# Modulation columns finished inside the large matmul loops, and filler matmuls with sink copies at four transitions of a two-block kernel

## The chip, the cores and the metric

One program runs on one core of a Trainium2 chip. The metric is the device time of an execution in microseconds (us); three executions of the kernel before took 2094.62, 2098.63 and 2100.15 us, so the median is 2098.63 us.

## The reference

Two transformer blocks stand behind each other, on one sequence of 256 tokens with 1024 features, all in float32. Each block first makes six modulation vectors of 1024 numbers from a conditioning vector, and uses them as shift, scale and gate:

```
mod = c @ w_mod + b_mod                # block 2: silu(c_2) @ w_ada_2 + b_ada_2
sh1, sc1, gt1, sh2, sc2, gt2 = split(mod, 6)
h  = rmsnorm(x, norm1_g) * (1 + sc1) + sh1
z  = h @ w_in                          # mixer: pooling, two kinds of attention, gates
x  = x + gt1 * (y @ w_out)             # y: what the mixer makes of z
h2 = rmsnorm(x, norm2_g) * (1 + sc2) + sh2
x  = x + gt2 * peer_ffn(h2)            # 16384 experts, all scored, 16 kept per head
```

Block 1 ends with a norm by `final_g`, and block 2 takes its result as `x`. So the norm at the end of block 1 and the norm at the head of block 2 follow directly on each other.

## The kernel before

The features of a token lie on the partitions in eight groups of 128 (`kk` 0 to 7). A product of two float32 matrices is made of three passes over a high and a low part of each (`hhi`, `hlo` for the activations, `hi`, `lo` for the weights), so every weight of 128x2048 that the SP queue loads into a raw buffer is split by ScalarE (L138, the high part) and VectorE (L141, the low part) before TensorE can use it. `Stream` keeps three raw buffers and three split buffers in one fixed order of units. The order of the instructions on each engine is the order in which the Python code records them: nothing is rescheduled afterwards, and every engine works through its own list in that order.

The time goes to four long stretches of matmuls: the mixer of block 1 (from 34 us to 228 us), its expert layer (235 us to 1042 us), the mixer of block 2 (1055 us to 1274 us) and its expert layer (from 1280 us). An expert layer writes the scores of the experts (`u` units, 128x256 matmuls, L442) and then the sums over them (`v` units, 128x512 matmuls, L897). Between the stretches lie four **transitions**, in which TensorE has little to do because a norm has to be worked out first:

- the **start**: `x` is loaded, normed, transposed (L552), and modulated by the first two modulation vectors into `hhi` and `hlo`;
- the **middle of block 1** and the **middle of block 2**, both at the end of `out_proj`: transposes of the new `x` (`turn`, L552), the rows' rsqrt (`norm_rows`), the spreading of it over the partitions (`spread_rows`, L516), then `modulate`, which makes eight products on VectorE (L533), eight high parts on ScalarE (L537) and eight low parts on VectorE (L524); TensorE's next matmuls (`mm_first`, L458 and L462) read them;
- the **seam of the blocks**, at the end of `peer` for block 1: the same, with two norms at once, in two groups of four `kk`, and with a new `xs` written in between (L1078); TensorE's next matmuls are L484.

A modulation vector is a sum over 1024 rows. VectorE adds the rows of the eight groups into one tile of 128x1024 (`mod_handler`, L332 and L334, tiles `macc` or `ringa`) while the weights stream by; TensorE then sums over the partitions with eight matmuls against a column of ones (`column`, L290; each is two records in the trace), and VectorE adds the bias (L300, and L303 for a scale). This last step is `finish_mod`. Finished tiles wait in the list `pending`, and `flush` takes them from its front after each unit, once they are three units old, but not those in `HOLD`, which wait for a transition (block and vector counted from 0):

```
HOLD = {(0, 3), (0, 4), (1, 1), (1, 0), (1, 2), (1, 3), (1, 4)}
while pending and pending[0][0] >= age and (age == 0 or pending[0][1] not in HOLD):
    finish_next()()
```

In the middle of block 1 two vectors are so finished, at the seam four, in the middle of block 2 one.

Of the kernel before, what the change touches and what calls it, by code (L numbers as in the profile page):

```python
# [9 lines left out]
F32 = mybir.dt.float32  # L10
# [30 lines left out]
RATE2 = 2  # L41
HOLD = {(0, 3), (0, 4), (1, 1), (1, 0), (1, 2), (1, 3), (1, 4)}

# [153 lines left out]
def kernel(  # L197
# [39 lines left out]

    # ---------------------------------------------------------- constants
    xpool = [ctx.enter_context(ExitStack())]
# [31 lines left out]

    # ---------------------------------------------------------- modulation
    modc = [keep.tile([128, 6, 8], F32, name=f"modc{b}") for b in range(2)]
# [4 lines left out]
    def mm_scratch():  # L278
        return ps_mm.tile([128, 512], F32, name="mm", tag="mm")
# [25 lines left out]

    def finish_next():
        age, bj, t, place, ps = pending.pop(0)
        del users[place]
        return finish_mod(*bj, t, ps)
# [33 lines left out]
    def flush(age=3):  # L343
        for p in pending:
            p[0] += 1
        while pending and pending[0][0] >= age and (age == 0 or pending[0][1] not in HOLD):
            finish_next()()

# [18 lines left out]

    # ---------------------------------------------------------- unit order
    last_v, first_v, xnext = [], [], []
# [55 lines left out]

    # ---------------------------------------------------------- helpers
    small = ctx.enter_context(tc.tile_pool(name="small", bufs=2))
# [48 lines left out]
    def mm_te(src, tick=None):  # L476
        ps = mm_tile()
        for p in range(2):
# [9 lines left out]
            if tick is not None:  # L488
                st.ahead()
                tick()  # L490
        return ps

    def rsqrt_seed(parts, base):
# [16 lines left out]
    def rsqrt_start(parts, base, v):  # L510
        return rsqrt_polish(rsqrt_seed(parts, base), v)
# [36 lines left out]
    def turn(xT, xs, i):  # L548
        for k in range(2):
            for tt in range(2):  # L550
                kk = 2 * i + k
                PE.transpose(xT[i][:, k, tt * 128:(tt + 1) * 128], xs[:, tt, kk * 128:(kk + 1) * 128], ident)  # L552
# [14 lines left out]
    def out_proj(b, yT, xs, gt, pool, at, rbt, ubuf):  # L567
# [37 lines left out]
        scale = finish_next()  # L605
        turn(xT, xs, tail[1])
        rb = norm_rows(ms, rbt, lambda: st.fill(2))
        scale()
        rest = [finish_next() for _ in range(len(pending))]
        modulate(b, 1, lambda kk: [(xT[kk // 2][:, kk % 2, :], slice(0, 256))], rb, ubuf,  # L610
                 first=lambda: [r() for r in rest] and rest.clear(), group=4)

    # ---------------------------------------------------------- PEER
    def peer(b, plan, keys_d, gelu, xs):
        with ExitStack() as px:
# [178 lines left out]
            with ExitStack() as gx:  # L794
# [253 lines left out]
                if b == 0:  # L1048
# [6 lines left out]
                    turn_x(1, 0)  # L1055
                    rest = [finish_next()]
                    scale()
                    turn_x(1, 1)
                    r = rsqrt_start([part[:, 0:1], part[:, 1:2]], base, v)
                    right.close()  # L1060
                    xnext.append(open_x())
                    st.fill(SPLIT_BUFS - 1)
                    rb = small.tile([128, S], F32, name="rb", tag="rb", bufs=1)
                    spread_rows(rb, r, psp.tile([128, 512], F32, name="g", tag="g"))
                    rest += [finish_next() for _ in range(len(pending))]
                    turns = [0, 1]
# [20 lines left out]

    # ---------------------------------------------------------- block 1 mixer
    with ExitStack() as mx:
# [43 lines left out]
        for _ in range(4):  # L1133
            st.process()
            st.settle()
        flush(0)
        sh, gs = modc[0][:, 0, :], modc[0][:, 1, :]
        for kk in range(8):
            A.activation(sga[:, kk, :], xT[kk // 2][:, kk % 2, :], AF.Copy, scale=gs[:, kk:kk + 1])
        for _ in range(3):  # L1140
            st.process()
            st.settle()
        st.fill(1)
        flush(0)
# [203 lines left out]

    # ---------------------------------------------------------- block 2 mixer
    with ExitStack() as mx:  # L1350
# [310 lines left out]
```

## Time and profile before

| | before |
|---|---|
| three executions, us | 2094.62, 2098.63, 2100.15 |
| median, us | 2098.63 |
| span of the profiled execution, first to last instruction, us | 2093.1 |
| median less that span, us | 5.5 |
| TensorE busy, us (share of the span) | 2050.3 (98%) |
| VectorE busy, us | 1603.1 (77%) |
| ScalarE busy, us | 986.8 (47%) |
| mean granted TensorE clock, of full speed | 0.989 |

The profile gives the span of the profiled execution and no time of its own beside it; the 5.5 us to the median stand for what lies around the span. "Busy" counts an instruction from its start to its end, and TensorE's instructions overlap, so 98% does not mean 98% of its peak. A number in brackets behind a row of the timeline is the time for which the engine had stood idle just before, with what ended the wait. The granted clock has two levels here, 1.00 (2.4 GHz) and 0.50 (1.2 GHz).

### The profile page before, as it was taken

How to read it: one execution, taken by the hardware profiler on the slowest of the kernel's cores; microseconds unless marked ns; L12 is line 12 of the kernel's file. 1: busy time of each engine (PE TensorE's matmuls, PEld its weight loads, DVE VectorE, ACT ScalarE, POOL GpSimd, SP SyncE). 2: the span in 40 equal slices, each digit the busy share in tenths (PEclk: the TensorE clock that was granted, in tenths of full speed). 3: DMA queues.
4: the chain of work that ended last, by engine and by line, in shares of the span. 5: the costliest groups of instructions: out<-in, count | busy, mean ns of one | idle time of the engine just before them, and what ended most of it. 6: DMA issues, size and time to landing. Idle time of an engine off the chain costs nothing.

```text
span 2093.1 us, 37810 instructions
## 1 busy us (share of the span) xinstructions
PE 2050.3 (98%) x15694; PEld 1885.9 (90%) x15694; DVE 1603.1 (77%) x2937; ACT 986.8 (47%) x1307; POOL 5.6 (0%) x15
## 2 busy tenths in 40 slices
PE   5999999999999999999999999999999999999998
PEld 4999999999999877888899999999999998778886
DVE  6787698868876799777668557988588766996556
ACT  4446455544344434444554455555443444344444
POOL 0000000000000000000000000000000000000000
PEclk8999999999999999999989999999999999999999
DMA  8555545554447644588445345555544475445563
GB/s 346 210 218 202 181 164 198 183 184 171 165 168 266 239 161 163 208 333 306 184 174 201 132 141 182 180 183 184 199 163 162 165 259 200 156 168 181 190 222 121
DMA packets 57211, 408.83 MB, mean 195 GB/s; under 512 B 6352, under 2 KB 6736, under 8 KB 8016
## 3 DMA queue, kind: packets, MB, share of 16 engines
q1 hardware_dynamic: 55424, 397.76, 53.4%
q0 software_dynamic: 1296, 8.52, 1.2%
q8 instruction: 123, 2.02, 0.4%
q14 instruction: 48, 0.39, 0.1%
q10 hardware_dynamic: 320, 0.14, 0.0%
HBM read 403.26 MB, written 3.15 MB: 194 GB/s over the span
## 4 chain that ended last, share of the span: by engine, by line
PE 91%; DVE 4%; ACT 2%; DMA 2%; issue 1%; SPq 0%; ACTq 0%; DVEq 0%
PE mm L442 46%; PE acc L897 31%; PE mm L484 2%; PE mm L580 2%; PE g L834 2%; PE g L835 1%; DVE lo L141 1%; PE acc L984 1%; DVE macc L334 1%; DMA raw<-in_w_in_dram 1%; ACT hi L138 1%; PE g L766 1%; PE acc L880 1%; PE mm L458 1%; PE mm L290 0%
## 5 line engine op out<-in xcount | busy, mean ns | idle before, releaser
L141 DVE TENSOR_TENSOR lo<-raw,hi 128x1024 fp32r<-128x1024 f32 x632 | 766.2, 1221 | 366.2 <-ACT hi L138 365.0
L138 ACT ACTIVATE hi<-raw 128x1024 fp32r<-128x1024 f32 x632 | 663.5, 1055 | 490.8 <-PE acc L897 226.5
L442 PE MATMUL mm<-hhi,hi 128*128 128x256 f32 x2848 | 399.8, 282 | 1.9 <-ACT sga L1330 1.6
L442 PE MATMUL mm<-hlo,hi 128*128 128x256 f32 x2848 | 392.9, 280 | 0.0
L442 PE MATMUL mm<-hhi,lo 128*128 128x256 f32 x2848 | 392.7, 280 | 0.0
L442 PEld LDWEIGHTS mm<-hhi,hi 128*128 128x128 f32 x2848 | 359.8, 188 | 6.2 <-ACT sga L1330 1.8
L442 PEld LDWEIGHTS mm<-hhi,lo 128*128 128x128 f32 x2848 | 358.0, 188 | 0.0
L442 PEld LDWEIGHTS mm<-hlo,hi 128*128 128x128 f32 x2848 | 357.9, 188 | 0.0
L897 PE MATMUL acc<-hi,whi 128*128 128x512 f32 x976 | 307.1, 396 | 0.7 <-ACT whi L545 0.7
L897 PE MATMUL acc<-lo,whi 128*128 128x512 f32 x976 | 301.9, 391 | 0.0
L897 PE MATMUL acc<-hi,wlo 128*128 128x512 f32 x976 | 300.6, 389 | 0.0
L897 PEld LDWEIGHTS acc<-hi,wlo 128*128 128x128 f32 x976 | 183.2, 188 | 39.6
L897 PEld LDWEIGHTS acc<-lo,whi 128*128 128x128 f32 x976 | 183.2, 188 | 39.1
L897 PEld LDWEIGHTS acc<-hi,whi 128*128 128x128 f32 x976 | 177.2, 188 | 33.5 <-ACT whi L545 1.6
L636 ACT ACTIVATE ringa<-mm 128x512 f32<-128x512 f32 x80 | 47.9, 599 | 111.6 <-PE mm L442 111.6
L827 DVE TENSOR_TENSOR gg<-b,gT 128x512 f16<-128x512 f16 x256 | 96.2, 417 | 0.0
L824 DVE TENSOR_TENSOR b<-iota,idx2T 128x1024 f16<-128x1024 f16 x128 | 87.5, 683 | 0.0
L545 ACT ACTIVATE whi<-ringa 128x512 fp32r<-128x512 f32 x78 | 48.8, 628 | 77.3 <-PE acc L897 77.3
L834 PEld LDWEIGHTS <-b 128*128 128x128 f16 x1024 | 63.4, 98 | 20.2 <-issue 8.3
L834 PE MATMUL g<-gg,b 128*128 128x64 f16 x1024 | 78.2, 194 | 0.1
L835 PE MATMUL g<-gg,b 128*128 128x64 f16 x1024 | 77.0, 193 | 0.0
L636 ACT ACTIVATE ringb<-mm 128x512 f32<-128x512 f32 x48 | 28.7, 599 | 93.8 <-PE mm L442 93.8
(359 smaller groups left out, 1837.5 us busy)
## 6 DMA issues: line engine op xcount, KB each, us to landing
raw<-in_peer_u_dram SPq DMA_DIRECT2D x128, 1024.0 KB, 4.9
raw<-in_peer_v_dram SPq DMA_DIRECT2D x118, 1024.0 KB, 4.9
raw<-in_w_in_dram SPq DMA_DIRECT2D x45, 1024.0 KB, 5.0
raw<-in_w_mod_dram SPq DMA_DIRECT2D x20, 1024.0 KB, 5.0
raw<-in_w_ada_dram SPq DMA_DIRECT2D x20, 1024.0 KB, 5.4
ringa<-in_peer_v_dram SPq DMA_DIRECT2D x10, 1024.0 KB, 5.6
raw<-in_w_out_dram SPq DMA_DIRECT2D x8, 1024.0 KB, 4.9
raw<-in_w_query_dram SPq DMA_DIRECT2D x8, 1024.0 KB, 4.9
```

What stands on the lines that cost most here:

```text
L138: self.nc.scalar.activation(hi, src, AF.Copy)
L141: self.nc.vector.tensor_sub(lo, src, hi.bitcast(F32))
L442: PE.matmul(ps[:, j, :], lhsT=w[:, k, :], rhs=h[:, k, :], start=n == 0 and k == 0, stop=n == 2 and k == 7)
L484: PE.matmul(ps[:, tt, :], lhsT=h[:, 4 * p + k, tt * 128:(tt + 1) * 128], rhs=w[:, k, :], start=p == 0 and tt == 0 and i == 0, stop=p == 1 ...
L545: A.activation(hi, src, AF.Copy)
L580: PE.matmul(acc[q][:, tt, :], lhsT=h[:, 4 * p + k, tt * 128:(tt + 1) * 128], rhs=w[:, k, :], start=p == 0 and tt == 0 and i == 0, stop=p = ...
L636: state["evac"] = lambda: A.activation(slots(p), ps, gelu)
L824: V.tensor_tensor(pairs(b2), lanes(0, 128), each(idx2T[:, c], 128), op=OP.is_equal)
L827: V.tensor_tensor(pairs(gg[:, :, i, :]), pairs(b1), each(gT[:, c, i, :], 64), op=OP.mult)
L834: PE.matmul(ps[:, t, :], lhsT=b2[:, t, :], rhs=gg[:, t, 0, :], start=True, stop=False)
L835: PE.matmul(ps[:, t, :], lhsT=b2[:, t, :], rhs=gg[:, t, 1, :], start=False, stop=True)
L897: PE.matmul(acc[tt][dh], lhsT=w[:, j, tt * 128:(tt + 1) * 128], rhs=v[:, dh * 512:(dh + 1) * 512], start=p == 0 and j == 0 and n == 0, sto ...
```

## The change

`HOLD` shrinks from seven vectors to three, and `flush` looks through the whole list instead of stopping at the first vector that has to wait. So (0, 3) is now finished in the mixer of block 1, and (1, 0), (1, 2) and (1, 3) among the `v` units of block 1. A new helper `busy` issues matmuls of 128x128 in float16 of `iota` against itself, 242 in all; their result is used nowhere. Behind the last of them at each transition VectorE copies one column of that result into a tile `junk`. Only comment lines are left out of the diff at the marks.

```diff
-HOLD = {(0, 3), (0, 4), (1, 1), (1, 0), (1, 2), (1, 3), (1, 4)}
+HOLD = {(0, 4), (1, 1), (1, 4)}
...
-    def finish_next():
-        age, bj, t, place, ps = pending.pop(0)
+    def finish_next(i=0):
+        age, bj, t, place, ps = pending.pop(i)
...
     def flush(age=3):
         for p in pending:
             p[0] += 1
-        while pending and pending[0][0] >= age and (age == 0 or pending[0][1] not in HOLD):
-            finish_next()()
+        for i in range(len(pending) - 1, -1, -1):
+            if pending[i][0] >= age and (age == 0 or pending[i][1] not in HOLD):
+                finish_next(i)()
...
+    def busy(ps, n):
+        for _ in range(n):
+            PE.matmul(ps[:, 0:128], lhsT=iota, rhs=iota, start=True, stop=True)
...
# out_proj, so the middle of both blocks
         turn(xT, xs, tail[1])
+        busy(rbt, 10)
         rb = norm_rows(ms, rbt, lambda: st.fill(2))
         scale()
+        idle = mm_scratch()
+        busy(idle, 24)
+        V.tensor_copy(small.tile([128, 1], F32, name="junk", tag="junk"), idle[:, 0:1])
         rest = [finish_next() for _ in range(len(pending))]
         modulate(b, 1, ...
...
# peer, block 1: the seam
                     turn_x(1, 0)
-                    rest = [finish_next()]
+                    rest = [finish_next() for _ in pending[:1]]
                     scale()
+                    idle = psp.tile([128, 512], F32, name="g", tag="g")
+                    rbt = psp.tile([128, 512], F32, name="g", tag="g")
+                    busy(idle, 24)
                     turn_x(1, 1)
+                    busy(idle, 12)
                     r = rsqrt_start([part[:, 0:1], part[:, 1:2]], base, v)
...
-                    spread_rows(rb, r, psp.tile([128, 512], F32, name="g", tag="g"))
-                    rest += [finish_next() for _ in range(len(pending))]
+                    spread_rows(rb, r, rbt)
+                    while pending:
+                        finish_next()()
+                    busy(idle, 36)
+                    V.tensor_copy(small.tile([128, 1], F32, name="junk", tag="junk"), idle[:, 0:1])
...
# block 1, the start
         flush(0)
+        idle = mm_scratch()
+        busy(idle, 90)
         sh, gs = modc[0][:, 0, :], modc[0][:, 1, :]
         for kk in range(8):
             A.activation(sga[:, kk, :], xT[kk // 2][:, kk % 2, :], AF.Copy, scale=gs[:, kk:kk + 1])
         for _ in range(3):
             st.process()
             st.settle()
+        busy(idle, 12)
+        V.tensor_copy(small.tile([128, 1], F32, name="junk", tag="junk"), idle[:, 0:1])
         st.fill(1)
         flush(0)
```

How the instructions move is shown at three places. First VectorE at the start: `macc_189` is the sum of the second modulation vector, `modc_97` the finished vectors of block 1. Before:

```order
L334 SCALAR_TENSOR_TENSOR macc_189<-raw,colt,macc_189 128x512
L334 SCALAR_TENSOR_TENSOR macc_189<-raw,colt,macc_189 128x512 [waits DVE_49]
L141 TENSOR_TENSOR lo<-raw,hi 128x1024 [waits DMAHW4_49,Activation_49]
L300 TENSOR_TENSOR modc_97<-at,colt 128x8 [waits PE_49]
L1148 TENSOR_SCALAR hhi<-sga,modc_97 128x256 [waits DVE_49]
```

and with the change:

```order
L334 SCALAR_TENSOR_TENSOR macc_189<-raw,colt,macc_189 128x512
L334 SCALAR_TENSOR_TENSOR macc_189<-raw,colt,macc_189 128x512 [waits DVE_49]
L1162 COPY junk<-mm 128x1 [waits PE_49]
L141 TENSOR_TENSOR lo<-raw,hi 128x1024 [waits DMAHW4_49,Activation_49]
L300 TENSOR_TENSOR modc_97<-at,colt 128x8
L1168 TENSOR_SCALAR hhi<-sga,modc_97 128x256 [waits DVE_49]
```

The wait for TensorE has moved from L300 to the copy, and the split L141 now stands behind it. Second, VectorE in the middle of block 1, from the last step of the rsqrt on. Before:

```order
L507 TENSOR_TENSOR rstd<-rstd,rt 128x2 [waits DVE_49]
L300 TENSOR_TENSOR modc_97<-at,colt 128x8 [waits PE_49]
L303 SCALAR_TENSOR_TENSOR modc_97<-modc_97,colt 128x8 [waits DVE_49]
L533 SCALAR_TENSOR_TENSOR sga<-at,modc_97,rb 128x256 [waits DVE_49,Activation_49]
L533 SCALAR_TENSOR_TENSOR sga<-at,modc_97,rb 128x256 x3
L300 TENSOR_TENSOR modc_97<-at,colt 128x8 [waits PE_49]
L533 SCALAR_TENSOR_TENSOR sga<-at,modc_97,rb 128x256 x4
```

and with the change:

```order
L512 TENSOR_TENSOR rstd<-rstd,rt 128x2 [waits DVE_49]
L300 TENSOR_TENSOR modc_97<-at,colt 128x8 [waits PE_49]
L303 SCALAR_TENSOR_TENSOR modc_97<-modc_97,colt 128x8 [waits DVE_49]
L617 COPY junk<-mm 128x1 [waits PE_49]
L538 SCALAR_TENSOR_TENSOR sga<-at,modc_97,rb 128x256 [waits DVE_49,Activation_49]
L538 SCALAR_TENSOR_TENSOR sga<-at,modc_97,rb 128x256 x7
```

The second L300 is gone from between the products (L533, now L538), and a copy that waits for TensorE stands ahead of all eight. In the middle of block 2 there was no second L300, and the same copy has come in; at the seam three L300 behind the first group of products are gone, and the copy (L1081) stands ahead of the first. Third, TensorE among the `v` units of block 1, where before there were only rows of L897 (now L906):

```order
L906 MATMUL acc_5557<-lo,whi 128x512
L906 MATMUL acc_5558<-lo,whi 128x512
L906 MATMUL acc_5557<-hi,wlo 128x512
L906 MATMUL acc_5558<-hi,wlo 128x512
L290 MATMUL mm<-ones,ringa 128x1 [waits PE_49]
L290 MATMUL mm<-ones,ringa 128x1 x7
L906 MATMUL acc_5555<-hi,whi 128x512 [waits Activation_49]
L906 MATMUL acc_5556<-hi,whi 128x512
```

Eight column matmuls have come in between two units; there are three such places, one for each moved vector of block 2.

## Rows read from the trace of the kernel before

**Rows 1.** The page, busy time of each engine in the whole span.

```profile
PE 2050.3 (98%) x15694; PEld 1885.9 (90%) x15694; DVE 1603.1 (77%) x2937; ACT 986.8 (47%) x1307; POOL 5.6 (0%) x15
```

**Rows 2.** Windows: length, busy us of PE, PEld, DVE, ACT, POOL; PEclk; DMA share, GB/s.

```profile
232.00:236.00 4.00, 3.20 (x19) 3.12 (x18) 2.85 (x8) 1.37 (x4) 0.00 (x0) 0.56 0.04 14
...
1280.00:1284.00 4.00, 4.00 (x20) 3.90 (x21) 4.00 (x12) 3.59 (x8) 0.00 (x0) 0.57 0.00 0
```

**Rows 3.** Timeline of TensorE, a column among the units: start, us, instructions.

```profile
681.02 1.84 PE L290 MATMUL mm<-ones,macc 128*128 128x1 f32 x16
682.72 0.72 PE L897 MATMUL acc<-hi,whi 128*128 128x512 f32 x2
```

**Rows 4.** Timeline of TensorE, mixer of block 1.

```profile
161.28 1.20 PE L442 MATMUL mm<-hhi,hi 128*128 128x256 f32 x8 [1.56 <-ACT sga L1330]
```

**Rows 5.** Timeline of TensorE, first float16 matmul of sixteen, and the row after them.

```profile
520.06 0.20 PE L834 MATMUL g<-gg,b 128*128 128x64 f16 x1
...
520.54 1.19 PE L442 MATMUL mm<-hhi,hi 128*128 128x256 f32 x8
```

**Rows 6.** Timeline of TensorE, middle of block 1.

```profile
231.66 0.40 PE L516 MATMUL at<-ident,rstd 128*128 128x128 f32 x2 [1.18 <-DVE modc L300]
231.90 2.87 PE L290 MATMUL at<-ones,macc 128*128 128x1 f32 x16
...
243.00 1.10 PE L442 MATMUL mm<-hhi,hi 128*128 128x256 f32 x8
```

**Rows 7.** Timeline of TensorE, middle of block 2.

```profile
1277.95 0.40 PE L516 MATMUL z<-ident,rstd 128*128 128x128 f32 x2 [1.17 <-DVE modc L300]
...
1279.89 0.39 PE L458 MATMUL mm<-hhi,hi 128*128 128x256 f32 x1 [1.53 <-ACT hhi L537]
...
1285.46 2.03 PE L462 MATMUL mm<-hlo,hi 128*128 128x256 f32 x16
1287.33 1.10 PE L442 MATMUL mm<-hhi,hi 128*128 128x256 f32 x8
```

**Rows 8.** Timeline of VectorE, middle of block 2.

```profile
1278.81 3.23 DVE L533 SCALAR_TENSOR_TENSOR sga<-at,modc,rb 128x256 f32<-128x256 f32 x8 [0.73 <-ACT rb L517]
```

**Rows 9.** Timeline of TensorE, seam of the blocks.

```profile
1047.48 0.66 PE L516 MATMUL g<-ident,rstd 128*128 128x128 f32 x2 [0.15 <-DVE rstd L507]
1047.93 6.83 PE L290 MATMUL mm<-ones,ringa 128*128 128x1 f32 x32
...
1062.81 0.63 PE L484 MATMUL mm<-hi,hhi 128*128 128x256 f32 x4
```

**Rows 10.** Timeline of VectorE, seam of the blocks.

```profile
1048.67 2.15 DVE L533 SCALAR_TENSOR_TENSOR fx<-xT,modc,rb 128x128 f32<-128x128 f32 x8
...
1054.79 0.17 DVE L300 TENSOR_TENSOR modc<-mm,colt 128x8 f32<-128x8 f32 x1 [3.25 <-PE mm L290]
...
1055.80 1.67 DVE L524 SCALAR_TENSOR_TENSOR hlo<-fx,modc,hhi 128x256 fp32r<-128x256 f32 x4
```

**Rows 11.** Timeline of ScalarE, seam of the blocks.

```profile
1050.93 1.70 ACT L537 ACTIVATE hhi<-fx,modc 128x256 fp32r<-128x256 f32 x4 [2.37 <-DVE modc L300]
...
1053.04 0.20 ACT L497 ACTIVATE rstd<-rstd 128x2 f32<-128x2 f32 x1
```

**Rows 12.** Timeline of TensorE, start.

```profile
29.19 3.57 PE L290 MATMUL at<-ones,macc 128*128 128x1 f32 x16 [7.70 <-DVE macc L334]
...
42.48 1.11 PE L1176 MATMUL at<-hhi,wfh 128*16 128x256 f32 x8 [1.00 <-ACT wfh L545]
```

**Rows 13.** Timeline of VectorE, start.

```profile
30.51 1.22 DVE L141 TENSOR_TENSOR lo<-raw,hi 128x1024 fp32r<-128x1024 f32 x1
32.80 0.17 DVE L300 TENSOR_TENSOR modc<-at,colt 128x8 f32<-128x8 f32 x1 [1.08 <-PE at L290]
...
35.75 1.23 DVE L141 TENSOR_TENSOR lo<-raw,hi 128x1024 fp32r<-128x1024 f32 x1
```

**Rows 14.** Timeline of the SP queue, start: a DMA issue.

```profile
37.38 0.43 SPq L1155 DMA_DIRECT2D wf<-in_w_f_dram  x1
```

## The prediction
> **What bounds the kernel now.** The busy times come first: TensorE is busy for 98% of the span and VectorE for 77% [rows 1], so only two things can change the time: work added to or taken from TensorE's long stretches, and the few places where TensorE waits or runs at half clock. The windows show that the granted clock is 0.56 and 0.57 in the middle of the two blocks [rows 2], a mix of its two levels of 1.2 and 2.4 GHz. What TensorE does there tells why the change may look promising: one-column matmuls, transposes and idle time. At half clock, 32 records of columns took 6.83 us at the seam, 0.213 each [rows 9]; inside a long stretch 16 took 1.70 us from their start to the next row's, 0.106 each [rows 3].
>
> The timelines then show who is waited for. In the middle of block 2, where no second vector is finished, 9.38 us lie between the rsqrt's spreading (L516) and the first L442 of the next stretch [rows 7]. In the middle of block 1 it is 11.34 us, because the columns of (0, 3) stand between [rows 6]. At the seam VectorE stands still for 3.25 us behind the columns of three vectors, and its low parts (L524) start only after that [rows 10]. So the transitions are chains through VectorE and ScalarE, in which the columns are an obstacle. In the long stretches TensorE itself is the chain.
>
> **The columns that move.** Each moved vector is 16 records. In a long stretch they push the next matmul back by 682.72 - 681.02 = 1.70 us [rows 3]; nothing stands idle there that could hide them. Three vectors go among the `v` units: 3 x 1.70 = **+5.1**. The fourth, (0, 3), lands in the mixer of block 1 just ahead of a wait of TensorE of 1.56 us for ScalarE's sigmoid [rows 4]. That wait ends when ScalarE has loaded a table behind work that doesn't depend on TensorE's last unit, so the column fits into it: 1.70 - 1.56 = **+0.1**. If the wait should move along instead, it is +1.7. VectorE's additions (L300, 0.17) are hidden in both places by its free quarter.
>
> **The price of a filler.** Before has no float16 matmul of 128 columns. The nearest are sixteen of 64 columns, which took 0.48 us up to the next row, 0.030 each [rows 5]; twice the columns make 0.060, which I take, for these have the same weight load and type. The lower bound is 0.030 (if the load sets the price), the upper one 0.117, from 16 matmuls of 256 columns in 1.87 us [rows 7]. The Trainium skill ("TensorE: Matmul & The Clock Gate", section "Back-to-back issue gap") says that a sustained stream of weight loads and matmuls of 128 columns runs at about 81 ns each; rows 5 have half that price at half the columns or less, and by 81 ns the sum below would be 2.0 us higher, about 2104.4.
>
> The fillers themselves stand where TensorE waits. But behind the last of them VectorE's copy into `junk` waits for TensorE, and VectorE works in its listed order: **what is queued behind that copy is the whole modulation.** So a filler is not free; it is late by as much as the copy outlasts the wait that was there anyway.
>
> **Middle of both blocks.** Count from the start of L516. The 24 fillers start at 0.24 (from L516 to the next row [rows 6]) and are issued by 0.24 + 24 x 0.060 = 1.68. The last one's result takes 0.20 - 0.06 more [rows 5], the copy about 0.13, so the products (L533) start at 1.95; before they started 0.86 after L516 in the middle of block 2 [rows 7, 8]. That is 1.1 us lost on the path. From there at full clock: 1.08 us to the first L458 [rows 7, 8]; seven more products at 3.23 / 8 = 0.40 [rows 8], 2.8 us, since each L458 pair needs one; 0.23 for the last pair; 1.87 for the second half of L458 and 1.87 for L462, both at 0.117 [rows 7]. Together 9.8 us. The low parts don't hold this up: at 1.67 / 4 = 0.42 each [rows 10] they end at 1.95 + 3.23 + 3.3 = 8.5, when L462 has just begun. Against 11.34 before that is **-1.5** in block 1, against 9.38 **+0.4** in block 2: there half the time at half clock is won and a little more is lost to the copy. The ten fillers ahead of L516 fit into the 1.18 and 1.17 us of waiting [rows 6, 7].
>
> **The seam.** L516 starts at 1047.48, 36 fillers end at 1047.72 + 2.16, and with the same 0.27 the products start at 1050.15 instead of 1048.67 [rows 9, 10]. They last 2.15, the last high part 1.70 / 4 = 0.42 longer [rows 11]: 1052.7. Before, that point was 1052.63, and ScalarE's second rsqrt ended 0.61 later, at 1053.24 [rows 11]; so now 1053.4. VectorE's part of it takes at most 1055.80 - 1054.79 - 0.17 = 0.84 [rows 10], and L524 starts at 1054.2 instead of 1055.80. Everything up to the first L484 of the second unit at 1062.81 [rows 9] hangs on this: **-1.6**. The 3.25 us wait is gone, but half of it comes back as the copy. The half clock here costs nothing by itself, as VectorE sets the pace.
>
> **The start.** TensorE is free from 29.19 - 7.70 = 21.5 on [rows 12]; 90 fillers take 5.4 us at full clock, 10.8 at half. The sum for the second vector ends at about 30.5, where L141 starts [rows 13]. Then come 8 records of columns, 12 fillers and the copy, and only then L141 (1.22), which until now ran while VectorE waited for the columns, and then L300. At full clock: 30.5 + 0.85 + 0.72 + 0.27 + 1.2 = 33.6 against 32.80 [rows 13], so 0.8 later; with half clock on columns and fillers 30.5 + 1.7 + 1.44 + 0.3 + 1.2 = 35.2, so 2.4 later. I take **+1.3**, nearer to the full clock, since the 90 fillers are dense work. TensorE's first unit would run faster at full clock, but that wins nothing: the next one (L1176) waits for `wf` already [rows 12], whose load is issued at 37.38 [rows 14], behind a load whose buffer the split from 35.75 to 36.98 sets free [rows 13]. That split is later by the same 1.3.
>
> **The sum.** 5.1 + 0.1 - 1.5 + 0.4 - 1.6 + 1.3 = +3.8 us on the profiled execution's span of 2093.1. What lies around the span (5.5 us to the median) doesn't change, so the median goes from 2098.6 to **2102.4 us**, 0.18% more. A measurement of this kernel tells about 0.3% (6.3 us) from no change, so I call it no change.
>
> **Rivals.**
> *Slower: the fillers don't hold the clock.* If the granted clock stays at half in the transitions, a filler costs 0.12 and L458 0.213. In the middle of a block the products then start at 0.24 + 2.88 + 0.3 = 3.4; first L458 at 4.5, its 32 matmuls 6.8, L462 1.9: 13.2 us, so +1.9 and +3.8. At the seam the copy is 2.2 later: +0.6. The start is +2.4. With 5.2 for the columns that is +13.9, 2112.5 us; from about two transitions on it decides for slower. For it: the clock fell at the seam and stayed low while TensorE was recorded as busy with columns without a break [rows 9]. Against: what fell was one-column work, and the fillers are dense matmuls. A price of 0.117 at full clock would do a like thing: 24 + 24 + 36 + 12 fillers at 0.057 more are +5.5, about 2108.
> *Slightly faster: the columns cost nothing among the `v` units.* If a wait that I don't see takes them up, as in the mixer, the sum is -1.3: 2097.3. Against it: the next row moved by the full 1.70 in the one case there is [rows 3].
> *Clearly faster: free columns, fillers at 0.030, and more half clock in other executions than in the profiled one.* Cheaper fillers give back 96 x 0.03 = 2.9, a middle of block 2 whose L462 also ran at half 1.5: -5.7, 2092.9. All three are needed.
> *The change doesn't do what it says:* if the three vectors still came last, at the seam, nothing but fillers and copies would be new. The listed order of TensorE excludes it.
>
> **How the numbers follow.** I give the forecast 0.62, slower fillers or a low clock 0.2, free columns 0.12, all that favours it together 0.06. The range has to reach from just under the free columns to the dear fillers, with two transitions at half clock: 2095 to 2110. Faster by over 0.3% is 0.07, slower by over 0.3% 0.2, between them 0.73.
>
> **What would show it.** In the changed profile, each step has its place: 1.70 us of L290 three times among the `v` units; the wait ahead of L442 near 161 us gone or under 0.3; clock 1.00 in all four transitions from the fillers on; VectorE idle ahead of each copy until TensorE's last filler, and the products 1.1 to 1.5 later after L516 than before; from L516 to the next L442 about 9.8 us in both blocks; `wf` issued later than 37.38. The forecast is wrong if the products don't start later, or if the `v` units take no longer.

## The result, and the profile after

The changed kernel took **2115.40 us** (median of four executions, 2114.09 to 2115.88), beside 2096.62 us for the kernel before on the same chip: a ratio of **1.0086, 95% interval 1.0072 to 1.0100**. It is slower by 0.9%, where no change was forecast, and lies above the range. The profiled execution of the changed kernel took 2115.34 us; its span is 2113.5 us, 20.4 more than before. So 1.8 us lie around the span here; of the 5.5 us that I had put there, most was that the profiled execution of before was shorter than the median.

The two traces can be cut at the same instructions and compared stretch by stretch (all from starts on TensorE; the second column from the rows before where they stand in a group):

| stretch | before, us | after, us | predicted | measured |
|---|---|---|---|---|
| start, to the first product with `wf` | 42.48 | 43.66 | +1.3 | +1.18 |
| mixer of block 1, to the spreading of the rsqrt | 189.18 | 190.55 | +0.1 | +1.37 |
| middle of block 1, from the spreading to the first L442 (now L443) | 11.34 | 9.81 | -1.5 | -1.53 |
| from there to the first `v` matmul of block 1 | 379.93 | 379.41 | 0 | -0.52 |
| **from the first `v` matmul of block 1 to the spreading at the seam** | 424.54 | 437.74 | +5.1 | **+13.19** |
| seam, from the spreading to the second unit | 15.33 | 14.26 | -1.6 | -1.08 |
| mixer of block 2, to the spreading of the rsqrt | 215.15 | 214.94 | 0 | -0.21 |
| middle of block 2, as in block 1 | 9.37 | 9.85 | +0.4 | +0.48 |
| from there to the first `v` matmul of block 2 | 379.90 | 379.36 | 0 | -0.54 |
| **from the first `v` matmul of block 2 to the last matmul** | 417.36 | 425.46 | 0 | **+8.10** |

So 16.2 of the 20.4 us (13.19 - 5.1 + 8.10) were lost where the change, beyond its three columns, does not touch a single instruction: among the `v` units, which alternate with `u` units in these two stretches. The busy times answer to [rows 1] and only hint at it, TensorE having 24 us more:

```profile
PE 2074.7 (98%) x15936; PEld 1893.1 (90%) x15936; DVE 1605.0 (76%) x2941; ACT 987.7 (47%) x1307; POOL 5.5 (0%) x15
```

The timeline shows it. Here is TensorE deep in the `v` units of block 2, first of the kernel before, then of the changed one (the columns are start, duration, engine, line, operation, output and inputs, where the moving operand stands ahead of the stationary one):

```profile
1980.51 0.62 PE L897 MATMUL acc<-hi,whi 128*128 128x512 f32 x2
1980.96 0.62 PE L897 MATMUL acc<-lo,whi 128*128 128x512 f32 x2
1981.42 0.61 PE L897 MATMUL acc<-hi,wlo 128*128 128x512 f32 x2
```

```profile
1979.94 0.63 PE L906 MATMUL acc<-hi,whi 128*128 128x512 f32 x2
1980.41 0.63 PE L906 MATMUL acc<-lo,whi 128*128 128x512 f32 x2
1980.87 0.63 PE L906 MATMUL acc<-hi,wlo 128*128 128x512 f32 x2
```

A pair of matmuls now follows the last after 0.465 us instead of 0.455. The median time from one start to the next went from 227 ns to 235 in block 1 and 234 in block 2 (the mean over both from 227.7 to 233.4), and nothing is idle between them. It is not the clock either. The windows of this stretch, before and after (length, TensorE's busy us and count, granted clock, DMA share, GB/s), have the full clock in both, and 222 matmuls against 215:

```profile
1950.00:2000.00 50.00, 50.00 (x222) 1.00 0.57 199
```

```profile
1950.00:2000.00 50.00, 50.00 (x215) 1.00 0.53 187
```

The two middles did what was forecast. The following lines are windows of the changed kernel (busy us of PE, PEld, DVE, ACT, POOL, then the granted clock): the middle of block 1, the seam, the middle of block 2 (the two middles answer to [rows 2]), and a place in the mixer of block 1 where the clock fell anew:

```profile
232.00:236.00 4.00, 3.33 (x45) 2.98 (x44) 1.46 (x11) 1.47 (x6) 0.00 (x0) 1.00 0.63 248
1066.00:1073.00 7.00, 6.64 (x26) 5.73 (x27) 5.91 (x20) 5.17 (x11) 0.00 (x0) 0.51 0.09 36
1290.30:1300.20 9.90, 8.64 (x74) 7.78 (x75) 7.77 (x19) 4.64 (x10) 0.95 (x2) 1.00 0.05 20
154.90:158.30 3.40, 3.40 (x19) 3.40 (x18) 3.37 (x13) 1.05 (x5) 0.00 (x0) 0.53 0.02 7
```

Both middles have the full clock now. TensorE in the middle of block 1, to hold against [rows 6]:

```profile
234.21 0.40 PE L521 MATMUL at<-ident,rstd 128*128 128x128 f32 x2 [0.63 <-DVE modc L300]
234.45 1.50 PE L496 MATMUL mm<-iota 128*128 128x128 f16 x24
237.15 0.39 PE L459 MATMUL mm<-hhi,hi 128*128 128x256 f32 x1 [1.20 <-ACT hhi L542]
...
242.16 2.03 PE L463 MATMUL mm<-hlo,hi 128*128 128x256 f32 x16
244.02 1.09 PE L443 MATMUL mm<-hhi,hi 128*128 128x256 f32 x8
```

and in the middle of block 2, to hold against [rows 7]:

```profile
1290.36 0.40 PE L521 MATMUL z<-ident,rstd 128*128 128x128 f32 x2 [0.63 <-DVE modc L300]
...
1293.30 0.39 PE L459 MATMUL mm<-hhi,hi 128*128 128x256 f32 x1 [1.20 <-ACT hhi L542]
...
1300.21 1.10 PE L443 MATMUL mm<-hhi,hi 128*128 128x256 f32 x8
```

VectorE in the middle of block 1, where the copy stands ahead of the products:

```profile
235.99 0.16 DVE L617 COPY junk<-mm 128x1 f32<-128x1 f32 x1 [1.65 <-PE mm L496]
236.07 3.23 DVE L538 SCALAR_TENSOR_TENSOR sga<-at,modc,rb 128x256 f32<-128x256 f32 x8
```

and at the seam, for [rows 10]:

```profile
1063.62 0.16 DVE L1081 COPY junk<-g 128x1 f32<-128x1 f32 x1 [1.18 <-PE g L496]
1063.69 2.15 DVE L538 SCALAR_TENSOR_TENSOR fx<-xT,modc,rb 128x128 f32<-128x128 f32 x8
...
1067.69 1.67 DVE L529 SCALAR_TENSOR_TENSOR hlo<-fx,modc,hhi 128x256 fp32r<-128x256 f32 x4
```

What remains is a suspicion with one clue. The change adds one more thing that is no instruction: the tile `junk`, two buffers of 32 bytes per partition in the pool `small`. Everything that is allocated behind it lies 64 bytes higher, the stationary operands `whi` and `wlo` of the `v` units among it. These are the start addresses in the built programs, in bytes within a partition, modulo 256:

| tile | role | before | after |
|---|---|---|---|
| `hi`, `lo` (three split buffers) | moving in `v`, stationary in `u` | 192 | 192 |
| `whi`, `wlo` | stationary in `v` | 192 | 0 |
| `yh`, `yl` | stationary in an out projection | 192 | 0 |
| `hhi`, `hlo` | moving in `u` | 224 | 224 |

The few units that use further split buffers are left out of the table: those buffers moved from 192 to 0 as well, which concerns 432 of the 8640 matmuls that read `hhi` or `hlo` as the moving operand, and 48 of the 192 with `yh` and `yl`. The pace of the matmuls with `yh` and `yl` changed too, and the other way: from 120 ns to 114 from one start to the next.

### The profile page after: what moved, and what is told of

The parts are those of the page before. It is cut to its first block, busy times and chain, and to the rows that moved or that the text cites. A ratio compares the mean times of both kernels' runs of the same rounds, so it can differ in the third digit from the quotient of the medians.

```text
span 2113.5 us, 38295 instructions
## 1 busy us (share of the span) xinstructions
PE 2074.7 (98%) x15936; PEld 1893.1 (90%) x15936; DVE 1605.0 (76%) x2941; ACT 987.7 (47%) x1307; POOL 5.5 (0%) x15
## 4 chain that ended last, share of the span: by engine, by line
PE 85%; issue 11%; DVE 2%; DMA 1%; ACT 1%; SPq 0%; POOLq 0%; DVEq 0%; ACTq 0%
PE mm L443 42%; PE acc L906 32%; PE g L843 2%; PE g L844 1%; PE mm L485 1%; PE acc L993 1%; DVE macc L334 1%; PE g L775 1%; PE acc L889 1%; PE mm L585 1%; DMA kT<-in_keys_dram 1%; PE mm L290 0%; DMA qT<-in_w_mod_dram 0%; PE at L1224 0%; PE at L1242 0%
## 5 line engine op out<-in xcount | busy, mean ns | idle before, releaser
L141 DVE TENSOR_TENSOR lo<-raw,hi 128x1024 fp32r<-128x1024 f32 x632 | 767.3, 1223 | 371.4 <-ACT hi L138 370.6
L443 PE MATMUL mm<-hhi,hi 128*128 128x256 f32 x2848 | 399.5, 283 | 0.3 <-ACT sqT L1535 0.3
L443 PE MATMUL mm<-hhi,lo 128*128 128x256 f32 x2848 | 393.1, 280 | 0.0
L443 PE MATMUL mm<-hlo,hi 128*128 128x256 f32 x2848 | 393.0, 280 | 0.0
L443 PEld LDWEIGHTS mm<-hhi,hi 128*128 128x128 f32 x2848 | 359.9, 188 | 4.6 <-issue 1.0
L443 PEld LDWEIGHTS mm<-hhi,lo 128*128 128x128 f32 x2848 | 358.9, 189 | 0.0
L443 PEld LDWEIGHTS mm<-hlo,hi 128*128 128x128 f32 x2848 | 358.7, 189 | 0.0
L906 PE MATMUL acc<-hi,whi 128*128 128x512 f32 x976 | 312.8, 402 | 0.6 <-ACT whi L550 0.6
L906 PE MATMUL acc<-lo,whi 128*128 128x512 f32 x976 | 307.1, 396 | 0.0
L906 PE MATMUL acc<-hi,wlo 128*128 128x512 f32 x976 | 306.9, 396 | 0.0
L906 PEld LDWEIGHTS acc<-hi,wlo 128*128 128x128 f32 x976 | 183.8, 188 | 44.0
L906 PEld LDWEIGHTS acc<-lo,whi 128*128 128x128 f32 x976 | 183.8, 188 | 43.7
L906 PEld LDWEIGHTS acc<-hi,whi 128*128 128x128 f32 x976 | 177.5, 189 | 37.7 <-ACT whi L550 1.5
```

What stands on the lines that cost most here:

```text
L141: self.nc.vector.tensor_sub(lo, src, hi.bitcast(F32))
L443: PE.matmul(ps[:, j, :], lhsT=w[:, k, :], rhs=h[:, k, :], start=n == 0 and k == 0, stop=n == 2 and k == 7)
L906: PE.matmul(acc[tt][dh], lhsT=w[:, j, tt * 128:(tt + 1) * 128], rhs=v[:, dh * 512:(dh + 1) * 512], start=p == 0 and j == 0 and n == 0, sto ...
```

## The experiments

Below, **distance** is the start of the moving operand less that of the stationary one, modulo 256 bytes. Before, it is 0 in the `v` units, 32 in the `u` units and 0 with `yh` and `yl`; in the changed kernel it is 192, 32 and 192 (without the few units just named).

**The tile, and the copies without it.** The copies stay, but write into a tile of the same shape that was there already:

```diff
-V.tensor_copy(small.tile([128, 1], F32, name="junk", tag="junk"), idle[:, 0:1])
+V.tensor_copy(epst, idle[:, 0:1])
```

> The changed kernel with the three copies written into the tile epst, which is there already and read by nobody; so the new tile junk is gone and every tile stands where it stood before the change. Theory A (the tile junk pushes whi and wlo, the stationary operands of the v units, 64 bytes up, and that slows their matmuls): 0.227 us from one v matmul to the next instead of 0.2335, and about 15.7 us less than the changed kernel, 2099 to 2102 us. Theory B (the slower v matmuls come from what the change adds to TensorE's list or to its clock): still 0.2335, about 2115 us.

It took 2104.43 us (2102.86 to 2105.68), ratio 1.0032 (1.0020 to 1.0043): 11 us less than the changed kernel, with the same instructions in the same order, where I had expected 15.7 less. The `v` units are back at 227 ns:

```profile
1979.81 0.62 PE L906 MATMUL acc<-hi,whi 128*128 128x512 f32 x2
1980.26 0.62 PE L906 MATMUL acc<-lo,whi 128*128 128x512 f32 x2
1980.72 0.61 PE L906 MATMUL acc<-hi,wlo 128*128 128x512 f32 x2
```

**Nothing but the shift.** The kernel before, with 64 unused bytes in the same pool:

```diff
+    V.memset(small.tile([128, 16], F32, name="pad", tag="pad", bufs=1), 0.0)
```

> The kernel before, with one tile of 64 bytes put into the pool small and written once, and nothing else. Theory A: v matmuls 0.2335 us apart, about 15 us slower than before, 2110 to 2113 us. Theory B: 0.227, no difference, 2097 us.

2108.32 us (2107.98 to 2110.56), ratio 1.0052 (1.0035 to 1.0069). The two stretches with `v` units are 8.60 and 8.07 us longer, and their matmuls have the changed kernel's pace:

```profile
1980.24 0.63 PE L898 MATMUL acc<-hi,whi 128*128 128x512 f32 x2
1980.71 0.63 PE L898 MATMUL acc<-lo,whi 128*128 128x512 f32 x2
1981.17 0.63 PE L898 MATMUL acc<-hi,wlo 128*128 128x512 f32 x2
```

So 64 bytes that no matmul reads cost 11 us: the shift makes the loss without any part of the change's logic. I had expected about 15. In the profiled execution the two stretches lose 16.7 us, and the rest of the span comes out 3.0 us shorter, 1.95 of it in the mixer of block 1; why is not shown.

**`whi` and `wlo` put back.** The changed kernel with 192 more bytes at the head of their pool, so that they are 256 bytes higher than before. The tiles behind them in the expert layers and at the seam (`b1`, `b2`, `gg` and a few more) move along; the tiles of the mixers, `yh` and `yl` among them, stay 64 bytes up:

```diff
+                V.memset(wk.tile([128, 48], F32, name="pad", tag="pad", bufs=1), 0.0)
```

> The changed kernel with a tile of 192 bytes at the head of the pool wk, so that whi and wlo stand 256 bytes above where they stood before the change, and everything else of the mixers 64 bytes above. Theory A, in the form that only whi and wlo matter for the v units and that 256 bytes make no difference: 0.227 us, the output projection's matmuls on yh stay at 0.114, 2098 to 2101 us. If another tile is the cause, or the absolute place: 0.2335, 2115 us.

2102.14 us (2100.07 to 2103.55), ratio 1.0020 (1.0010 to 1.0030). `v` is at 227 ns again, `yh` and `yl` keep 114:

```profile
1980.17 0.62 PE L907 MATMUL acc<-hi,whi 128*128 128x512 f32 x2
1980.62 0.62 PE L907 MATMUL acc<-lo,whi 128*128 128x512 f32 x2
1981.08 0.61 PE L907 MATMUL acc<-hi,wlo 128*128 128x512 f32 x2
```

So the loss in the `v` units comes from `whi` and `wlo` or from a tile that moved along with them, and 256 bytes make no difference; that it is the two operands, the map below shows, where no other tile is used. Against the run with `epst`, which has the old addresses, this one is 2.3 us faster (2102.14 against 2104.43). That is not all the other tiles' shift: in the profiled executions 1.2 us of it lie in the middle of block 1, where the clock fell to half in the run with `epst` and not here.

**The copies taken away.** The changed kernel without its three copies and so without `junk`; nothing reads the fillers' result:

```diff
-        V.tensor_copy(small.tile([128, 1], F32, name="junk", tag="junk"), idle[:, 0:1])
```

> The changed kernel without its three copies (the fillers stay, their result is read by nobody). Tiles stand as before the change. If the copy holds up the modulation as predicted: products 0.86 us after the spreading instead of 1.86 in the middle of both blocks, 1.2 us earlier at the seam, L300 at the start 0.5 to 1 earlier; against the kernel with the copies in epst 3 to 5 us less. If another wait takes the copy's place: no difference between the two.

2097.47 us, ratio 0.9999 (0.9989 to 1.0009). The copies cost 7 us against the run with the copies in `epst`. VectorE in the middle of block 1 now waits for the spread rsqrt alone, which is ready well before the fillers end:

```profile
234.10 3.23 DVE L538 SCALAR_TENSOR_TENSOR sga<-at,modc,rb 128x256 f32<-128x256 f32 x8 [0.73 <-ACT rb L522]
```

The products start 0.85 us after TensorE's L521 at 233.25 instead of 1.86. The middles of both blocks take 8.81 us, the seam 12.20, the start 42.16. Against the changed kernel that is 1.0, 1.0, 2.1 and 1.5 us. The run with `epst` lost more in the middles (11.03 and 11.17 us), because there the granted clock fell to half for 3.4 us in each, although its list of instructions is that of the changed kernel. These are windows of that run within its two middles (columns as above):

```profile
237.00:242.00 5.00, 5.00 (x26) 4.69 (x27) 5.00 (x13) 2.73 (x6) 0.03 (x1) 0.66 0.00 0
1288.00:1293.00 5.00, 5.00 (x25) 4.59 (x26) 5.00 (x13) 2.76 (x6) 0.00 (x0) 0.66 0.00 0
```

Why it fell in the one and not in the other stays open. Each kernel has one profiled execution, and executions of one and the same kernel differ in this: over the ten of the run with `whi` put back the mean granted clock went from 0.993 (2103.55 us) to 0.997 (2100.07 and 2100.45 us). So a fall that one trace has and another has not is no proof of a difference between their kernels.

**The list of finished vectors alone.** New `HOLD` and `flush`, no fillers, no copies:

```diff
-HOLD = {(0, 3), (0, 4), (1, 1), (1, 0), (1, 2), (1, 3), (1, 4)}
+HOLD = {(0, 4), (1, 1), (1, 4)}
```

> Only the new HOLD and flush, no fillers and no copies, all addresses as before. Theory (the terms of the sum hold, each at its place): three columns among the v units of block 1 +5.1 us; the column in the mixer 0 to +1.7; middle of block 1 about 9.4 us as block 2 had, -2.0; seam about 12.5 to 13, -2.5; middle of block 2 and start as before: +0.6 to +2.3, about 2098.5 us. Rival (the fillers give the clock that pays for the columns, and without them the transitions win nothing): middle of block 1 at 11 us, seam at 15, 2102 us or more.

2098.95 us (2097.51 to 2100.76), ratio 1.0009 (0.9999 to 1.0018). Its stretches: `v` of block 1 +5.5, middle of block 1 9.12 us (-2.2), seam 13.17 (-2.2), mixer of block 1 +1.7, middle of block 2 +1.1. The expected terms came close, except that the middle of block 2, where nothing was expected, lost 1.1 us with half clock for 6.8 us, and the two sides nearly cancel. Neither this ratio nor its difference from the run without copies is clear of noise.

**Which address matters: a map.** A kernel that does nothing but matmuls of the large stretches' forms on constants, 64 pairs of offsets for each of three forms (`y_like` has 256 columns like `u_like`, with other stationary operands in turn, and gave the same map within 0.1 ns on the mean):

```diff
+    for f in (u_like, y_like, v_like):
+        for w in range(0, 64, 8):
+            for x in range(0, 64, 8):
+                f(pp.tile([128, 512], F32, name="ps", tag="ps"), w, x)
```

> The whole two-block computation is left out: the kernel only runs matmuls of the forms of the large stretches on constants, 16 for each pair of offsets, with the stationary operand and the moving operand each shifted by 0 to 224 bytes in steps of 32 against a multiple of 256 (64 pairs for each of three forms). Theory (the start address of one operand sets the price of a matmul): the 128x512 form shows two levels near 227 and 233.5 ns that follow the shift of one operand alone, 64 bytes apart, and the forms of 256 columns show 114 and 120 where two stationary tiles alternate. Rival (the distance between the two operands decides, as when both are read from the same place at once): the levels follow the difference of the two shifts, and a shift of both changes nothing. Second rival (other traffic into the same memory, from VectorE, ScalarE or DMA, makes the difference): with no other engine at work all 64 pairs of a form have one interval, near 216 for 512 columns and 109 for 256.

The mean ns from one start to the next, over the eight pairs of each distance (16 matmuls a pair), and the lowest and highest of the eight:

```
distance, bytes     0      32     64     96     128    160    192    224
128x512 (v)       227.7  233.5  229.3  233.2  233.1  234.1  233.1  232.9
  lowest          227.0  233.4  228.6  233.1  232.2  233.9  232.6  232.6
  highest         228.2  233.6  230.0  233.4  233.3  234.1  233.6  233.1
128x256 (u)       119.6  118.0  117.8  119.3  118.9  117.5  115.0  118.1
  lowest          119.4  116.9  117.7  119.1  118.4  117.2  113.6  117.9
  highest         120.0  118.2  117.9  120.1  119.1  118.8  117.8  118.4
```

My theory was wrong here and its rival right: it is not the address of one operand, but the distance between the two. A shift of both by the same bytes changes little, at most 2 ns, except for 256 columns at distance 192, where the eight pairs lie between 113.6 and 117.8. No other engine works while these matmuls run, so the paces need no other engine's traffic. Distance 0 is best for 512 columns and worst for 256; that is why the same 64 bytes slowed `v` and sped up `yh`. And the `u` units, at 32, don't have their best distance.

**The map tried in the kernel.** An unused tile in the pool of `hhi` and `hlo` puts these lower, and with them only the distance of the matmuls that read these two changes, which are the `u` units and, with the two as stationary operands, 624 others; in the `u` units 24 floats give 192, 8 floats give 0, 32 floats give 160:

```diff
+    V.memset(hpool.tile([128, 24], F32, name="hpad"), 0.0)
```

> The kernel before with one unused tile of 96 bytes in the pool of hhi and hlo, which puts both 96 bytes lower: in the u units the moving operand then starts 192 bytes (mod 256) behind the stationary one instead of 32; the operands of the v units keep their distance of 0. Theory (the distance between the start addresses of the two operands, mod 256, sets the interval, and the map of the measurement without the computation holds inside the kernel): u matmuls go from 117 to between 114 and 115 ns, v matmuls stay at 227; over 8500 u matmuls that is 20 to 27 us less, 2070 to 2078 us in all. Rival (only the address of the stationary operand counts, which the weights in their rings keep): 2097 us, u at 117 ns. Second rival (the map doesn't carry over, because other engines and DMA use the memory too): between 2085 and 2100.

> The same with 32 bytes in place of 96, so that hhi, hlo and the weights start at the same place mod 256, distance 0. Theory (distance): u matmuls at 120 ns, 2.5 to 3 ns dearer, so 20 to 26 us more, 2117 to 2124 us, while v, for which 0 is the best distance, stays at 227. Rival (stationary address alone): 2097 us.

> The kernel before with 128 bytes in place of 96 in the pool of hhi and hlo, distance 160 in the u units. Theory (distance, map of the measurement without the computation: 117 ns on the mean): u matmuls within 0.7 ns of before (116.99), 2092 to 2102 us. Rival (lower hhi is better as such): at or under the 2083 us of the 96 bytes.

Distance 192: 2083.14 us (2079.20 to 2084.16), ratio 0.9921 (0.9904 to 0.9937). Distance 0: 2119.19 us, ratio 1.0096 (1.0079 to 1.0112). Distance 160: 2106.93 us, ratio 1.0048 (1.0029 to 1.0067). The mean over the `u` matmuls is 116.99 ns before, 115.29, 119.81 and 118.08 in the three; times some 8,500 matmuls that is -14.5, +24 and +9.3 us, against -14.8, +21.3 and +9.7 in the medians (before was 2097.9 and 2097.21). The pace at distance 0 can be read off the row of eight, 0.96 us:

```profile
620.09 1.12 PE L443 MATMUL mm<-hhi,lo 128*128 128x256 f32 x8
621.05 1.12 PE L443 MATMUL mm<-hlo,hi 128*128 128x256 f32 x8
```

So the distance sets the time inside the kernel too. But two of the three times missed what I expected: the gain at 192 is smaller (2083 us, not 2070 to 2078), and 160 came out dearer (118.1 ns where the map's mean has 117.5; 2107 us, not 2092 to 2102). At 192 the trace shows why: there are two levels. First a stretch at 113 ns (eight in 0.90 us), then one at 118 (eight in 0.94), with `v` units between:

```profile
615.23 1.07 PE L443 MATMUL mm<-hhi,lo 128*128 128x256 f32 x8
616.13 1.07 PE L443 MATMUL mm<-hlo,hi 128*128 128x256 f32 x8
617.04 0.63 PE L898 MATMUL acc<-hi,whi 128*128 128x512 f32 x2
...
622.49 1.10 PE L443 MATMUL mm<-hhi,hi 128*128 128x256 f32 x8
623.44 1.11 PE L443 MATMUL mm<-hhi,lo 128*128 128x256 f32 x8
624.38 1.10 PE L443 MATMUL mm<-hlo,hi 128*128 128x256 f32 x8
```

At 160 there are two as well, nearer to each other: in block 1 a run of 816 `u` matmuls without a break went at 117.3 ns, one of 384 at 118.6.

**Both gains together.** The changed kernel without copies, `hhi` and `hlo` 96 bytes lower, once with the two tiles from above as well (64 bytes in `small`, 192 at `whi`), once without:

> The changed kernel without its three copies, with hhi and hlo 96 bytes lower, a 64-byte tile at the head of the small pool (yh and yl at 0 mod 256) and a 192-byte tile at the head of the pool of whi and wlo (these back at 192). Theory (distance): 2097.5 less the gain of the u units (20 to 27 us) and 2 us of the matmuls with yh and yl: 2069 to 2076 us, v at 227 ns. Rival (stationary address alone): 2095 us.

> The changed kernel without its three copies and with hhi and hlo 96 bytes lower, and no other tile added: it differs from the run with all three tiles only in where the small tiles, the matrices of the mixer and the operands of the out projections lie. Theory (the two gains add up, and which of its two levels, 113.4 or 117.8 ns, the u matmuls take at a distance of 192 hangs on what comes before them on TensorE, whose list is the same as in that run): levels mostly at 117.8 again, 2086 to 2090 us. Rival (traffic of the other engines, whose addresses moved, sets the level): more of the units at 113.4 as with u_spread, 2080 to 2085 us.

With them 2087.16 us, ratio 0.9943 (0.9926 to 0.9960), 11 us above the expected range, and the `u` matmuls at 116.23 ns on the mean; without them **2081.09 us** (2079.35 to 2081.98), ratio 0.9918 (0.9901 to 0.9934), at 115.08. The second is better than both kernels, but can't be told from the one tile of 96 bytes in the kernel before. My expectation for it, that TensorE's list of work fixes the level, missed by 5 us: two kernels with the same list spent different shares at the two levels. The largest difference is the run of 816 `u` matmuls in each block: all at 117.8 ns with the tiles, all at 113.3 without them. The rival's time, 2080 to 2085 us, came true; whether its cause did, the traffic of the other engines, no run here separates.

**The two levels by themselves.** Again without the computation, groups of 48 `u`-like matmuls with `v`-like ones between:

```diff
+    for x in (48, 8, 0):
+        for n in (0, 24, 23, 22, 1):
+            for i in range(12):
+                u(48, x)
+                v(n, 0)
```

> The computation is left out: twelve groups of 48 u-like matmuls each at distances 192, 32 and 0, with 0, 24, 23, 22 or 1 v-like matmuls between the groups, nothing else running. Theory (the level at 192 is taken over from what comes before on TensorE and kept to the end of a group): at 192 each group is at 113.4 or at 117.8 from its first matmuls to its last, groups behind v-like matmuls mostly at 117.8, and the uninterrupted twelve at 113.4 throughout; at 32 and 0 one level, 117 and 120. Rival (it is the traffic of the other engines): 113.4 in all groups at 192.

TensorE from 17 us on, all at distance 192, first without interruption, then behind `v`-like matmuls:

```profile
16.73 69.18 PE L248 MATMUL ps<-X,W 128*128 128x256 f32 x609
85.75 5.62 PE L254 MATMUL acc<-X,W 128*128 128x512 f32 x24
91.20 5.82 PE L248 MATMUL ps<-X,W 128*128 128x256 f32 x48
96.86 5.60 PE L254 MATMUL acc<-X,W 128*128 128x512 f32 x24
```

Uninterrupted, the groups ran at (85.75 - 16.73) / 609 = 113.3 ns. The first group behind `v`-like matmuls took (96.86 - 91.20) / 48 = 117.9 ns, and from there all groups did, also with a single `v`-like matmul between them. At 32 it is 116.7 and at 0 120.0 in every group (119.8 at the least). So at 192 the level hangs on what ran before and is then kept while `u`-like matmuls follow each other, with no other engine at work. What brings back 113 in the kernel stays open. In the three kernels at distance 192 all 192 groups of `u` matmuls that stand behind the short float16 matmuls ran at 113.3 ns, and 45 of the 48 behind a `v` unit at 117.8; neither order was tried by itself.

## Why the prediction was wrong

**The step that failed** is the one that was never priced: that what the change does not touch stays as it is. The `v` units stand in the sum with three columns, +5.1, and with nothing in block 2. The columns cost just that. This is the first of the three that moved, 1.71 us from its first matmul to the next row; the other two, at 982.88 and 1030.34, took 1.70 each:

```profile
936.29 1.84 PE L290 MATMUL mm<-ones,ringa 128*128 128x1 f32 x16
938.00 0.71 PE L906 MATMUL acc<-hi,whi 128*128 128x512 f32 x2
```

But the copy was priced as an instruction of 0.13 us, and not as a tile. The tile moved two operands by 64 bytes, and 3 x 976 matmuls of L906 became 16.2 us / 2928 = 5.5 ns dearer. By the ratios (times 2097 us) the change splits into four, each from two kernels that differ in it alone: `HOLD` and `flush` +1.9 us, fillers -2.1, copies +6.9, the addresses +11.3; together +18.0. The 95% intervals of these ratios reach about 0.001 to either side, 2 us, so only the copies and the addresses are clear of noise. The last is a balance: putting `whi` and `wlo` back won 13.3 us (2115.40 to 2102.14), and what remains of it, 2.3 us the other way, is the difference between the run with `epst` and this one.

**The rest of the sum held, with some luck.** Without the 16.2 us it comes to +4.2 where I had +3.8. That is closer than its terms: the mixer came out 1.3 above its term and the seam 0.5, while the three stretches that I had at 0 came out 1.3 shorter together. The run without the tile took 2104.43 us, 2 us from the forecast and within the range, but that is luck too: against 2097.2 us for the kernel before on its chip it is +7.2, and the 2098.6 from which I had counted was high.
- *Filler:* 0.060 was taken. 24 of them lasted 1.50 us with the last one's 0.20, so (1.50 - 0.20) / 23 = 0.057. The Trainium skill's 81 ns ("TensorE: Matmul & The Clock Gate", section "Back-to-back issue gap") is not what this case shows.
- *Middles:* 9.81 and 9.85 us, 9.8 forecast; the products start 1.86 us after L521 (1.95 forecast), the first L459 1.08 later, and the clock is full. The copy does lose what the clock wins in block 2.
- *Seam:* the copy, and L529 6.52 us behind L521 (6.7 forecast, 8.32 before). From there to the second unit it takes 7.73 us instead of 7.01, with a granted clock of 0.66 instead of 0.81 on that way. I had called half clock free at the seam; by this it was not quite, by 0.7.
- *Start:* +1.18 for +1.3, and `wf` was issued at 38.57 instead of 37.38, as the chain through the split has it. The clock was at half from 21.6 to 25.0 and from 31.8 to 38.6 us, though, where I had looked for full clock from the fillers on.
- *Mixer:* the wait ahead of 161.28 [rows 4] is gone, as forecast, but the stretch lost 1.37 and not 0.1. The half clock in 154.9 to 158.3 is what is new, right behind the moved column's one-column matmuls, which follow small matmuls of the attention:

```profile
152.10 1.95 PE L290 MATMUL at<-ones,macc 128*128 128x1 f32 x16
153.91 1.43 PE L443 MATMUL mm<-hhi,hi 128*128 128x256 f32 x8
155.14 1.91 PE L443 MATMUL mm<-hhi,lo 128*128 128x256 f32 x8
156.84 1.67 PE L443 MATMUL mm<-hlo,hi 128*128 128x256 f32 x8
158.36 0.59 PE L1224 MATMUL at<-cst,lf 128*128 128x256 f32 x2
```

The column fits into the wait, as forecast; what the stretch lost is the half clock, 24 matmuls in 4.45 us here. The runs with `HOLD` alone and without copies have it too (+1.7 and +1.9), the ones with `epst` and with `whi` put back have not (+0.2 and +0.5). Of the seven profiled kernels with that column three show the fall, one execution each; what decides it stays open.

**The rivals.** "Slower: the fillers don't hold the clock" gave 2112.5 us, nearer to 2115.4 than my forecast. It was right by accident: the clock was full in both middles, and the run with the old addresses, with all fillers and half clock for 3.4 us in each middle, took 2104. A time that fits is no proof of its mechanism. Free columns are refuted by the three columns at 936.29, 982.88 and 1030.34; that the change doesn't do what it says, by the same rows.

**Why the change wins nothing even at the old addresses.** Moving four vectors out of the transitions wins 2.2 us in the middle of block 1 and 2.2 at the seam, and pays 5.5 among the `v` units, where TensorE has no gap, and 1.7 in the mixer, where the clock fell. The fillers win back about 2, which is not clear of noise. The copies, which only make the fillers count as read, stand ahead of the modulation and cost 7.

## What to carry to other kernels

A new tile is a change to every tile behind it: before costing an edit, compare the start addresses of the large matmuls' operands in the two built programs, and where a stretch that wasn't touched changes its pace, look there first. With fp32r matmuls back to back it pays to choose the distance of the two operands on purpose: one unused tile of 96 bytes won 0.8% here, while the change at the old addresses and without its copies came out even. Work that is added to fill an engine's wait should not be read by an engine that is on the path.

## What the runs showed of the hardware that was not expected

- The pace of back-to-back fp32r matmuls hangs on the distance of the operands' start addresses modulo 256 bytes: 227 to 234 ns for 512 columns (best at 0), 113.3 to 120 for 256 columns (best at 192, worst at 0), at full granted clock and with no other engine at work.
- At distance 192 the 256-column form has two paces, 113.3 and 117.8 ns; which one holds hangs on the matmuls before, and it lasted through hundreds of matmuls (a run of 816 at 113.3 or at 117.8).
- Two programs with the same list of instructions, which differ in addresses alone, had half clock in different transitions of their profiled executions: the changed kernel none in the middles, the one with `epst` 3.4 us in each. That the addresses decide it is not shown, since executions of one kernel differ in their mean clock too (0.993 to 0.997 in ten of the run with `whi` put back).
